# Five of eight row pairs with seven products in the feed-forward blocks of a two-layer decoder trunk

## The chip, the cores and the metric

The kernel runs on one core of a Trainium2 chip. The metric is the device time of one execution in microseconds (us); less is better. Engines are named as the profile names them: PE (TensorE, matmuls), DVE (VectorE), ACT (ScalarE), POOL (GpSimd) and SP (the engine that issues the transfers).

## The reference

A decoder trunk of two layers on 256 tokens of width 2048, all float32. Layer 0 mixes tokens with an mLSTM, layer 1 with an RG-LRU; behind each mixer stands a SwiGLU feed-forward block of inner width 5632, and a norm ends the trunk. The change lies in the feed-forward blocks:

```python
def swiglu(x, w_in, w_out):
    g, u = jnp.split(x @ w_in, 2, axis=-1)
    return (jax.nn.silu(g) * u) @ w_out

for layer in range(DEPTH):
    ...
    h = h + mix
    h = h + swiglu(rms_norm(h, norm_ffn[layer]), ffn_w_in[layer], ffn_w_out[layer])
return rms_norm(h, norm_final)
```

## The kernel before

Every float32 factor is kept as two halves: a high half, rounded by ACT (`hi`, L235), and a low half, the remainder made by DVE (`lo`, L236). A product of two factors is three matmuls, high by high, high by low and low by high, into the same accumulator (`product`, L752 to L755, one line for each).

`ffn` (L732) computes the feed-forward block of a layer in 11 blocks j of 512 inner columns. `inner` (L757) makes gate and up columns of a block for both halves of the tokens: `pairs` (L259) loads w_in in 8 row pairs p (two 128-row slices, gate and up columns, so a raw tile of 4 x 512 columns, two transfers of 512 KB), and each pair is a 2 x 2 by 2 x 2 block product. A plain pair does it in 8 products (24 matmuls). A pair in `SEVENS` does it in 7 products (21 matmuls, `PRODUCTS`, L35): for these, DVE first makes four sums of weight blocks into the one tile `sum` (L274, L277, L278), then both the three raw blocks that are used as they are (tiles `whix`, `wlox`, 1536 columns) and the four sums (`whit`, `wlot`, 2048 columns) are split into halves (`halves`, L238). The token side has its sums ready in tiles `p_f` (`NormPairs.pair`, L412), made once per layer while the mixer's output projection runs. Block 0 takes pairs 2 and 3 plainly (`BOTH`, L32), with additional token tiles from the pool `more`, since its pairs follow each other with nothing between them.

The halves lie in three high and three low tiles in rotation (`four`, L223); a plain pair takes one of each, a pair with seven products takes two. Raw tiles are also three in rotation, `sum` is one. So the tile of a pair's sums can be written when PE has read the raw blocks of the pair before, and the tile of raw blocks when PE has read the sums two tiles earlier.

Between the products of the pairs, PE does output pieces: `outs` (L816) multiplies the finished inner block j - 1 by w_out in 8 pieces of 12 matmuls, and `between` (L868) places one in each pair, from pair 4 of block j to pair 3 of block j + 1; so pairs 0 to 3 of block 1 have none of their own. A piece's weights are split by ACT and DVE too (`whio`, `wloo`), and ACT copies the residual into the accumulator (L855) and back (L862). At pair 6, the last with seven products, DVE and ACT combine the accumulators into gate and up (L787 to L801).

A scheduler sets each engine's order when the kernel is built: instructions in the program's order by readiness, those under `high_priority` earlier. Each engine then works through its order in sequence, waiting on semaphores; a waiting instruction holds up what stands behind it on its engine.

Of the kernel before, what the change touches and what calls it, by code (L numbers as in the profile page):

```python
# [28 lines left out]

SEVENS = (2, 3, 5, 6)  # L30

BOTH = (2, 3)  # L32

# [9 lines left out]
def kernel(  # L43
# [193 lines left out]

    def halves(name, src, n=4):  # L238

        hi, lo = four("whi", name, F32R, 3), four("wlo", name, F32R, 3)  # L240
        split(hi[:, 0:n, :], lo[:, 0:n, :], src[:, 0:n, :])
        return [(hi[:, i, :], lo[:, i, :]) for i in range(n)]
# [16 lines left out]
    def pairs(w, j):  # L259

        wv = w.rearrange("(k p) n -> p k n", p=P)
        for p in range(NK // 2):
# [9 lines left out]
            with tc.high_priority(offset=AHEAD):  # L272
                t = four("sum", f"{j}_{p}", F32, 1)
                nc.vector.tensor_tensor(  # L274
                    t[:, 0:2, :], raw[:, 1:3, :], raw[:, 3:4, :].broadcast_to([P, 2, NB]), op=ALU.add
                )
                nc.vector.tensor_tensor(t[:, 2, :], t[:, 0, :], raw[:, 2, :], op=ALU.add)  # L277
                nc.vector.tensor_tensor(t[:, 3, :], t[:, 2, :], raw[:, 0, :], op=ALU.add)  # L278
                both = halves(f"x{j}_{p}", raw, 3) + halves(f"t{j}_{p}", t)
            yield p, dict(zip(("B21", "B11", "B22", "T1", "T3", "T2", "T4"), both))  # L280
# [124 lines left out]
    class NormPairs(Norm):  # L405
# [6 lines left out]
        def pair(self, p):  # L412
# [7 lines left out]
            place, tag = ("c", "c") if "c" in pools else ("rawo", "raw0")  # L420
            c = pool_of(place).tile([P, 11 if place == "c" else 8, P], F32, tag=tag, name=f"c_{self.name}{p}")
            for k, sl in ((k0, slice(0, 2)), (k1, slice(2, 4))) if plain else ((k0, slice(1, 3)), (k1, slice(0, 4, 3))):
# [4 lines left out]
            else:  # L427

                nc.vector.tensor_tensor(
                    c[:, 4:6, :], c[:, 0:1, :].broadcast_to([P, 2, P]), c[:, 2:4, :], op=ALU.subtract  # L430
                )
                nc.vector.tensor_tensor(c[:, 6, :], c[:, 3, :], c[:, 4, :], op=ALU.subtract)
# [8 lines left out]
            if p in BOTH:  # L441

                nc.scalar.copy(c[:, 8, :], c[:, 0, :])
                nc.vector.tensor_tensor(c[:, 9, :], c[:, 1, :], c[:, 2, :], op=ALU.subtract)
                nc.vector.tensor_tensor(c[:, 10, :], c[:, 3, :], c[:, 0, :], op=ALU.subtract)
                more = pool_of("more").tile([P, 2, 3, P], F32R, tag=f"m{p}", name=f"m{p}_{self.name}")
                split(more[:, 0], more[:, 1], c[:, 8:11, :])
                self.more[p] = more
# [16 lines left out]
        def plain(self, p, f):  # L465

            x = self.x[p]
            if p not in self.more:
                return [(x[:, 0, i, :], x[:, 1, i, :]) for i in (2 * f, 2 * f + 1, 4 + f)]
            m = self.more[p]  # L470
            return [
                (t[:, 0, i, :], t[:, 1, i, :]) for t, i in (((x, 0), (x, 1), (m, 1)), ((x, 2), (m, 0), (m, 2)))[f]
            ]
# [258 lines left out]
    def ffn(layer, n, nxt):  # L732
# [24 lines left out]
        def inner(j, between):  # L757
# [12 lines left out]
            for p, ops in pairs(w, j):  # L770
# [14 lines left out]
                if p == SEVENS[-1]:  # L785
                    with tc.high_priority(offset=AHEAD):
                        nc.scalar.copy(s0, ps["P1"])  # L787
                        nc.vector.tensor_tensor(d0, ps["Q6"], s0, op=ALU.subtract)
                        nc.vector.tensor_tensor(d1, ps["P7"], d0, op=ALU.add)
            with tc.high_priority(offset=AHEAD):  # L790
                nc.vector.tensor_tensor(d0, ps["Q5"], d0, op=ALU.add)
                nc.vector.tensor_tensor(s1, ps["Q5"], d1, op=ALU.add)
                nc.vector.tensor_tensor(s0, ps["P2"], s0, op=ALU.add)
                nc.scalar.activation(s0, s0, AF.Silu, scale=n.rstd[:, 0:1])
                nc.vector.tensor_tensor(d0, ps["Q3"], d0, op=ALU.add)
                nc.vector.tensor_tensor(d1, ps["P4"], d1, op=ALU.subtract)
                nc.scalar.activation(d1, d1, AF.Silu, scale=n.rstd[:, 1:2])
# [317 lines left out]
```

## Time and profile before

| | |
|---|---|
| median of 3 runs | 2118.57 us (2117.81 to 2119.58) |
| the profiled execution's own time | 2118.39 us |
| its span, first to last instruction | 2116.6 us |
| PE busy | 2099.8 us, 99% |
| DVE busy | 1584.5 us, 75% |
| ACT busy | 1274.6 us, 60% |
| read from HBM | 401.84 MB, 191 GB/s over the span |

An engine's busy time is the union of its instructions' times. Matmuls overlap, so PE's busy share doesn't tell how far apart they are issued; for that the starts in the timeline, or the count of matmuls in a stretch, are read. Idle time of an engine that isn't waited for costs nothing. The stretches by stage: block 0 of the first feed-forward runs from 402.9 us, block 1 from 447.2, block 2 from 500.4, and from there each block takes 63.5 to 63.7 us; the second feed-forward begins at 1402.3 us and repeats the pattern.

### The profile page before, as it was taken

The page shows a single profiled execution, that of the slowest core. Times are in us where ns is not written, and L with a number is a line of the kernel's source. Part 1 is how long each engine was busy: PE and PEld are TensorE (multiplying, and loading weights), DVE is VectorE, ACT ScalarE, POOL GpSimd, SP SyncE. Part 2 cuts the span into 40 slices and gives each one's busy share as a digit, 9 for nine tenths or more (in the row PEclk, how much of TensorE's full clock was granted, in tenths as well). Part 3 has the DMA queues.
Part 4 walks back from the last instruction along what each step waited for, and adds up shares of the span by engine and source line. Part 5 has one row for each costly group of instructions (what it writes and reads, how often), then busy time and mean ns, then how long its engine had stood idle before and what let it go on. Part 6 is the DMA issues. An engine that isn't in the chain of part 4 may idle for free.

```text
span 2116.6 us, 27325 instructions
## 1 busy us (share of the span) xinstructions
PE 2099.8 (99%) x10604; PEld 1777.5 (84%) x10604; DVE 1584.5 (75%) x1610; ACT 1274.6 (60%) x1452; POOL 43.2 (2%) x62
## 2 busy tenths in 40 slices
PE   9999999999999999999999999999999999999998
PEld 8988888878888888888889999787888888888886
DVE  6655556688787787887776786868877877887875
ACT  5444445556666656666665758655756666666664
POOL 0011110000000000000000000000000000000002
PEclk9999999999999999999999999999999999999999
DMA  7556666556566565565545666765666655666653
GB/s 214 166 163 178 180 179 219 199 179 199 201 217 199 180 203 194 199 219 197 178 162 161 195 191 182 230 202 174 202 204 211 203 180 194 196 206 215 200 178 120
DMA packets 211082, 405.73 MB, mean 192 GB/s; under 512 B 14520, under 2 KB 14728, under 8 KB 210824
## 3 DMA queue, kind: packets, MB, share of 16 engines
q1 hardware_dynamic: 210808, 402.94, 59.0%
q8 instruction: 83, 1.36, 0.3%
q10 hardware_dynamic: 144, 1.05, 0.1%
q14 instruction: 47, 0.39, 0.0%
HBM read 401.84 MB, written 2.10 MB: 191 GB/s over the span
## 4 chain that ended last, share of the span: by engine, by line
PE 96%; ACT 2%; DVE 1%; issue 1%; DMA 0%; SPq 0%; ACTq 0%; POOLq 0%; POOL 0%; DVEq 0%
PE P L753 8%; PE out L753 8%; PE P L755 8%; PE P L754 8%; PE out L754 8%; PE out L755 8%; PE Q L754 7%; PE Q L755 7%; PE Q L753 7%; PE po L291 2%; PE po L292 2%; PE po L290 2%; PE qk L307 1%; PE qk L308 1%; PE qk L309 1%; PE v L290 1%
## 5 line engine op out<-in xcount | busy, mean ns | idle before, releaser
L211 DVE TENSOR_TENSOR wlo<-raw,whi 128x1024 fp32r<-128x1024 f32 (+1 forms) x225 | 273.1, 1217 | 179.9 <-ACT whi L210 178.7
L210 ACT CAST whi<-raw 128x1024 fp32r<-128x1024 f32 (+1 forms) x225 | 234.6, 1047 | 202.9 <-PE po L292 42.4
L236 DVE TENSOR_TENSOR wlot<-sum,whit 128x2048 fp32r<-128x2048 f32 x84 | 192.5, 2292 | 147.3 <-ACT whit L235 147.3
L753 PE MATMUL out<-whio,hh 128*128 128x512 f32 x704 | 275.0, 391 | 0.0
L754 PE MATMUL out<-wloo,hh 128*128 128x512 f32 x704 | 274.3, 390 | 0.0
L755 PE MATMUL out<-whio,hh 128*128 128x512 f32 x704 | 273.3, 389 | 0.0
L235 ACT CAST whio<-rawo 128x1024 fp32r<-128x1024 f32 (+1 forms) x166 | 183.7, 1106 | 126.5 <-PE out L755 119.1
L862 ACT COPY h<-out 128x512 f32<-128x512 f32 x154 | 90.2, 586 | 252.5 <-PE out L755 252.5
L236 DVE TENSOR_TENSOR wlo<-raw,whi 128x2048 fp32r<-128x2048 f32 x92 | 210.3, 2288 | 32.0 <-ACT whi L235 31.4
L236 DVE TENSOR_TENSOR wloo<-rawo,whio 128x1024 fp32r<-128x1024 f32 (+1 forms) x166 | 210.9, 1282 | 3.6 <-ACT whio L235 3.0
L235 ACT CAST whit<-sum 128x2048 fp32r<-128x2048 f32 x84 | 160.5, 1911 | 74.2 <-DVE sum L278 36.0
L235 ACT CAST whi<-raw 128x2048 fp32r<-128x2048 f32 x92 | 175.6, 1916 | 29.5 <-DMA raw<-in_ffn_w_in_dram 18.5
L236 DVE TENSOR_TENSOR wlox<-raw,whix 128x1536 fp32r<-128x1536 f32 x84 | 147.3, 1753 | 47.8 <-ACT whix L235 47.8
L753 PEld LDWEIGHTS out<-whio,hh 128*128 128x128 f32 x704 | 132.2, 188 | 28.9 <-ACT out L855 0.9
L755 PEld LDWEIGHTS out<-whio,hh 128*128 128x128 f32 x704 | 132.2, 188 | 27.8
L754 PEld LDWEIGHTS out<-wloo,hh 128*128 128x128 f32 x704 | 132.2, 188 | 27.2
L753 PE MATMUL P<-whi,p_f 128*128 128x512 f32 x364 | 141.9, 390 | 1.6 <-ACT whi L235 1.6
L755 PE MATMUL P<-whi,p_f 128*128 128x512 f32 x364 | 141.9, 390 | 0.0
L754 PE MATMUL P<-wlo,p_f 128*128 128x512 f32 x364 | 141.6, 389 | 0.0
L753 PE MATMUL Q<-whi,p_f 128*128 128x512 f32 x356 | 140.6, 396 | 0.2 <-DVE h L485 0.2
L754 PE MATMUL Q<-wlo,p_f 128*128 128x512 f32 x356 | 138.8, 390 | 0.0
L755 PE MATMUL Q<-whi,p_f 128*128 128x512 f32 x356 | 138.6, 389 | 0.0
(284 smaller groups left out, 4819.0 us busy)
## 6 DMA issues: line engine op xcount, KB each, us to landing
raw<-in_ffn_w_in_dram SPq DMA_DIRECT2D x352, 512.0 KB, 4.9
rawo<-in_ffn_w_out_dram SPq DMA_DIRECT2D x176, 512.0 KB, 4.3
raw<-in_m_w_in_dram SPq DMA_DIRECT2D x95, 512.0 KB, 3.8
raw<-in_r_w_in_dram SPq DMA_DIRECT2D x64, 512.0 KB, 3.8
raw<-in_m_w_out_dram SPq DMA_DIRECT2D x32, 512.0 KB, 3.7
raw<-in_r_w_out_dram SPq DMA_DIRECT2D x32, 512.0 KB, 3.9
gr<-in_r_gate_w_dram SPq DMA_DIRECT2D x8, 512.0 KB, 3.9
h<-in_x_dram SPq DMA_DIRECT2D x4, 512.0 KB, 7.7
```

The lines of the kernel that those rows point to most:

```text
L210: nc.scalar.copy(hi[:, i:i + step, 0:ncols], r)
L211: nc.vector.tensor_tensor(lo[:, i:i + step, 0:ncols], r, hi[:, i:i + step, 0:ncols].bitcast(F32), op=ALU.subtract)
L235: nc.scalar.copy(hi, src)
L236: nc.vector.tensor_tensor(lo, src, hi.bitcast(F32), op=ALU.subtract)
L290: nc.tensor.matmul(o, lhsT=ah[:, bs], rhs=hi, start=(k == 0), stop=False)
L291: nc.tensor.matmul(o, lhsT=ah[:, bs], rhs=lo, start=False, stop=False)
L292: nc.tensor.matmul(o, lhsT=al[:, bs], rhs=hi, start=False, stop=(k == nk - 1))
L307: nc.tensor.matmul(o, lhsT=hi, rhs=ah, start=first_in_bank, stop=False, skip_group_check=True)
L753: nc.tensor.matmul(o, lhsT=a[0], rhs=b[0], start=start, stop=False, **kw)
L754: nc.tensor.matmul(o, lhsT=a[0], rhs=b[1], start=False, stop=False, **kw)
L755: nc.tensor.matmul(o, lhsT=a[1], rhs=b[0], start=False, stop=stop, **kw)
L862: nc.scalar.copy(hs, o)
```

## The change

Pair 4 joins the pairs with seven products in all blocks but block 0, where it stays plain, like pairs 2 and 3, from tiles in `more`. The low and high halves of the four sums are made in two parts of two sums each (`step=2`): T1 and T3 first, then T2 and T4. On the token side the difference that two products share is kept with the other sign (A7), so that one tile less is needed in `more`, and the signs of `d1` are turned to match.

```diff
--- before.py
+++ after.py
@@ -27,9 +27,9 @@
 BIG = 1e30
 AHEAD = 1000
 
-SEVENS = (2, 3, 5, 6)
-
-BOTH = (2, 3)
+SEVENS = (2, 3, 4, 5, 6)
+
+BOTH = (2, 3, 4)
 
 SHIFT = 48
 PRODUCTS = (
@@ -235,10 +235,12 @@
         nc.scalar.copy(hi, src)
         nc.vector.tensor_tensor(lo, src, hi.bitcast(F32), op=ALU.subtract)
 
-    def halves(name, src, n=4):
+    def halves(name, src, n=4, step=4):
 
         hi, lo = four("whi", name, F32R, 3), four("wlo", name, F32R, 3)
-        split(hi[:, 0:n, :], lo[:, 0:n, :], src[:, 0:n, :])
+        for i in range(0, n, step):
+            at = slice(i, min(n, i + step))
+            split(hi[:, at, :], lo[:, at, :], src[:, at, :])
         return [(hi[:, i, :], lo[:, i, :]) for i in range(n)]
 
     def stream4(w, c0, nk):
@@ -276,7 +278,7 @@
                 )
                 nc.vector.tensor_tensor(t[:, 2, :], t[:, 0, :], raw[:, 2, :], op=ALU.add)
                 nc.vector.tensor_tensor(t[:, 3, :], t[:, 2, :], raw[:, 0, :], op=ALU.add)
-                both = halves(f"x{j}_{p}", raw, 3) + halves(f"t{j}_{p}", t)
+                both = halves(f"x{j}_{p}", raw, 3) + halves(f"t{j}_{p}", t, step=2)
             yield p, dict(zip(("B21", "B11", "B22", "T1", "T3", "T2", "T4"), both))
 
     def linear_tok(w, c0, nk, act, name, ncols=NB, lag=0):
@@ -418,7 +420,7 @@
             for i, (k, b) in enumerate(order):
                 nc.tensor.transpose(pt[:, i, :], h[:, b, k * P:(k + 1) * P], ident)
             place, tag = ("c", "c") if "c" in pools else ("rawo", "raw0")
-            c = pool_of(place).tile([P, 11 if place == "c" else 8, P], F32, tag=tag, name=f"c_{self.name}{p}")
+            c = pool_of(place).tile([P, 10 if place == "c" else 8, P], F32, tag=tag, name=f"c_{self.name}{p}")
             for k, sl in ((k0, slice(0, 2)), (k1, slice(2, 4))) if plain else ((k0, slice(1, 3)), (k1, slice(0, 4, 3))):
                 nc.scalar.activation(c[:, sl, :], pt[:, sl, :], AF.Copy, scale=self.gain[:, k:k + 1])
             if plain:
@@ -426,9 +428,8 @@
                 src = c[:, 0:6, :]
             else:
 
-                nc.vector.tensor_tensor(
-                    c[:, 4:6, :], c[:, 0:1, :].broadcast_to([P, 2, P]), c[:, 2:4, :], op=ALU.subtract
-                )
+                nc.vector.tensor_tensor(c[:, 4, :], c[:, 0, :], c[:, 2, :], op=ALU.subtract)
+                nc.vector.tensor_tensor(c[:, 5, :], c[:, 3, :], c[:, 0, :], op=ALU.subtract)
                 nc.vector.tensor_tensor(c[:, 6, :], c[:, 3, :], c[:, 4, :], op=ALU.subtract)
                 nc.vector.tensor_tensor(c[:, 7, :], c[:, 1, :], c[:, 6, :], op=ALU.subtract)
                 src = c[:, 1:8, :]
@@ -442,9 +443,8 @@
 
                 nc.scalar.copy(c[:, 8, :], c[:, 0, :])
                 nc.vector.tensor_tensor(c[:, 9, :], c[:, 1, :], c[:, 2, :], op=ALU.subtract)
-                nc.vector.tensor_tensor(c[:, 10, :], c[:, 3, :], c[:, 0, :], op=ALU.subtract)
-                more = pool_of("more").tile([P, 2, 3, P], F32R, tag=f"m{p}", name=f"m{p}_{self.name}")
-                split(more[:, 0], more[:, 1], c[:, 8:11, :])
+                more = pool_of("more").tile([P, 2, 2, P], F32R, tag=f"m{p}", name=f"m{p}_{self.name}")
+                split(more[:, 0], more[:, 1], c[:, 8:10, :])
                 self.more[p] = more
 
         def parts(self, q):
@@ -469,7 +469,7 @@
                 return [(x[:, 0, i, :], x[:, 1, i, :]) for i in (2 * f, 2 * f + 1, 4 + f)]
             m = self.more[p]
             return [
-                (t[:, 0, i, :], t[:, 1, i, :]) for t, i in (((x, 0), (x, 1), (m, 1)), ((x, 2), (m, 0), (m, 2)))[f]
+                (t[:, 0, i, :], t[:, 1, i, :]) for t, i in (((x, 0), (x, 1), (m, 1)), ((x, 2), (m, 0), (x, 4)))[f]
             ]
 
     def bc2(ap):
@@ -786,14 +786,15 @@
                     with tc.high_priority(offset=AHEAD):
                         nc.scalar.copy(s0, ps["P1"])
                         nc.vector.tensor_tensor(d0, ps["Q6"], s0, op=ALU.subtract)
-                        nc.vector.tensor_tensor(d1, ps["P7"], d0, op=ALU.add)
+
+                        nc.vector.tensor_tensor(d1, ps["P7"], d0, op=ALU.subtract)
             with tc.high_priority(offset=AHEAD):
                 nc.vector.tensor_tensor(d0, ps["Q5"], d0, op=ALU.add)
-                nc.vector.tensor_tensor(s1, ps["Q5"], d1, op=ALU.add)
+                nc.vector.tensor_tensor(s1, ps["Q5"], d1, op=ALU.subtract)
                 nc.vector.tensor_tensor(s0, ps["P2"], s0, op=ALU.add)
                 nc.scalar.activation(s0, s0, AF.Silu, scale=n.rstd[:, 0:1])
                 nc.vector.tensor_tensor(d0, ps["Q3"], d0, op=ALU.add)
-                nc.vector.tensor_tensor(d1, ps["P4"], d1, op=ALU.subtract)
+                nc.vector.tensor_tensor(d1, ps["P4"], d1, op=ALU.add)
                 nc.scalar.activation(d1, d1, AF.Silu, scale=n.rstd[:, 1:2])
                 for b, (u, g) in enumerate(((d0, s0), (s1, d1))):
                     nc.vector.scalar_tensor_tensor(
```

What the built order of instructions shows at three places (a name carries the tile's kind, then block and pair, then a buffer number: `wlot8_5` is the low half of the sums of pair 5 in block 8):

DVE in an ordinary block, first before, from the sums of pair 5 on:

```order
L274 TENSOR_TENSOR sum8_5_7492<-raw8_5_7489 128x1024
L277 TENSOR_TENSOR sum8_5_7492<-sum8_5_7492,raw8_5_7489 128x512
L278 TENSOR_TENSOR sum8_5_7492<-sum8_5_7492,raw8_5_7489 128x512
L236 TENSOR_TENSOR wlo8_4_7435<-raw8_4_7431,whi8_4_7434 128x2048
L236 TENSOR_TENSOR wlox8_5_7497<-raw8_5_7489,whix8_5_7496 128x1536
L236 TENSOR_TENSOR wloo700_7458<-rawo700_7456,whio700_7457 128x1024
L236 TENSOR_TENSOR wloo701_7464<-rawo701_7462,whio701_7463 128x1024
L236 TENSOR_TENSOR wlot8_5_7501<-sum8_5_7492,whit8_5_7500 128x2048
```

and with the change, from the sums of pair 4 on:

```order
L276 TENSOR_TENSOR sum8_4_7557<-raw8_4_7554 128x1024
L279 TENSOR_TENSOR sum8_4_7557<-sum8_4_7557,raw8_4_7554 128x512
L280 TENSOR_TENSOR sum8_4_7557<-sum8_4_7557,raw8_4_7554 128x512
L236 TENSOR_TENSOR wlox8_4_7562<-raw8_4_7554,whix8_4_7561 128x1536
L236 TENSOR_TENSOR wlot8_4_7566<-sum8_4_7557,whit8_4_7565 128x1024 x2
L236 TENSOR_TENSOR wloo700_7588<-rawo700_7586,whio700_7587 128x1024
L276 TENSOR_TENSOR sum8_5_7622<-raw8_5_7619 128x1024
L236 TENSOR_TENSOR wloo701_7594<-rawo701_7592,whio701_7593 128x1024
L279 TENSOR_TENSOR sum8_5_7622<-sum8_5_7622,raw8_5_7619 128x512
L236 TENSOR_TENSOR wlox8_5_7627<-raw8_5_7619,whix8_5_7626 128x1536
L280 TENSOR_TENSOR sum8_5_7622<-sum8_5_7622,raw8_5_7619 128x512
L236 TENSOR_TENSOR wlot8_5_7631<-sum8_5_7622,whit8_5_7630 128x1024 x2
```

The single 2048-wide split of pair 4 has become three sums, a 1536-wide split and two 1024-wide splits, and every `wlot` is now two instructions.

PE at the end of block 0, from the first product with the sums of pair 6 (`P7`, `Q5`, `Q6`, `P4` are accumulators), before:

```order
L753 MATMUL P7_0_3881<-whit0_6_3906,p6_f0_3708 128x512
L753 MATMUL Q5_0_3669<-whit0_6_3906,p6_f0_3708 128x512
L753 MATMUL Q6_0_3888<-whit0_6_3906,p6_f0_3708 128x512
L753 MATMUL P4_0_3690<-whit0_6_3906,p6_f0_3708 128x512
L753 MATMUL P2_0_3676<-whi0_7_3937,p7_f0_3751 128x512
L754 MATMUL P7_0_3881<-wlot0_6_3907,p6_f0_3708 128x512
L755 MATMUL P7_0_3881<-whit0_6_3906,p6_f0_3708 128x512
L754 MATMUL Q5_0_3669<-wlot0_6_3907,p6_f0_3708 128x512
```

and with the change:

```order
L753 MATMUL P7_0_3893<-whit0_6_3918,p6_f0_3718 128x512
L754 MATMUL P7_0_3893<-wlot0_6_3919,p6_f0_3718 128x512
L755 MATMUL P7_0_3893<-whit0_6_3918,p6_f0_3718 128x512
L753 MATMUL Q5_0_3678<-whit0_6_3918,p6_f0_3718 128x512
L754 MATMUL Q5_0_3678<-wlot0_6_3919,p6_f0_3718 128x512
L755 MATMUL Q5_0_3678<-whit0_6_3918,p6_f0_3718 128x512
L753 MATMUL Q6_0_3900<-whit0_6_3918,p6_f0_3718 128x512
L754 MATMUL Q6_0_3900<-wlot0_6_3919,p6_f0_3718 128x512
```

Before, the four products begin with the high half alone, and a matmul of pair 7 stands ahead of the first low half; now each product runs its three matmuls in sequence.

ACT in an ordinary block, around the copies of an output piece (`L862`, later `L863`), before:

```order
L235 CAST whi8_4_7434<-raw8_4_7431 128x2048
L235 CAST whix8_5_7496<-raw8_5_7489 128x1536
L235 CAST whio700_7457<-rawo700_7456 128x1024
L862 COPY h_73<-out631_7407 128x512
L235 CAST whio701_7463<-rawo701_7462 128x1024
L855 COPY out700_7468<-h_73 128x512
L235 CAST whit8_5_7500<-sum8_5_7492 128x2048
```

and with the change, in block 7, where the rotation of the three tiles stands differently:

```order
L235 CAST whix7_4_7075<-raw7_4_7068 128x1536
L235 CAST whit7_4_7079<-sum7_4_7071 128x1024
L235 CAST whio600_7101<-rawo600_7100 128x1024
L863 COPY h_73<-out531_7044 128x512
L235 CAST whit7_4_7079<-sum7_4_7071 128x1024
L235 CAST whio601_7107<-rawo601_7106 128x1024
L856 COPY out600_7112<-h_73 128x512
L235 CAST whix7_5_7140<-raw7_5_7133 128x1536
```

In that block the second part of the copy of pair 4's sums stands behind the copy of output piece `out531`; in the blocks beside it both parts stand ahead of it.

## Rows read from the trace of the kernel before

**Rows 1.** The page: busy time by engine, and the chain by engine.

```profile
PE 2099.8 (99%) x10604; PEld 1777.5 (84%) x10604; DVE 1584.5 (75%) x1610; ACT 1274.6 (60%) x1452; POOL 43.2 (2%) x62
...
PE 96%; ACT 2%; DVE 1%; issue 1%; DMA 0%; SPq 0%; ACTq 0%; POOLq 0%; POOL 0%; DVEq 0%
```

**Rows 2.** Busy time by stretch: block 1, block 8, its pairs 2 to 6.

```profile
core 0: us, PE busy (x) PEld busy (x) DVE busy (x) ACT busy (x) POOL busy (x), PEclk, DMA share, GB/s
...
447.20:500.40 53.20, 53.20 (x238) 43.19 (x236) 48.19 (x42) 31.81 (x30) 0.00 (x0) 1.00 0.59 195
881.97:945.62 63.65, 63.65 (x285) 52.52 (x284) 51.21 (x44) 40.55 (x42) 0.00 (x0) 1.00 0.61 198
899.45:937.49 38.04, 38.04 (x169) 31.27 (x168) 30.31 (x22) 25.84 (x25) 0.00 (x0) 1.00 0.64 203
```

**Rows 3.** Timelines (start, duration, engine, line, [idle before, releaser]): block 8, pair 6.

```profile
926.94 2.29 DVE L236 TENSOR_TENSOR wlot<-sum,whit 128x2048 fp32r<-128x2048 f32 x1 [0.71 <-ACT whit L235]
...
932.50 0.39 PE L754 MATMUL P<-wlot,p_f 128*128 128x512 f32 x1
```

**Rows 4.** Timelines: block 1, sums of pairs 3, 5 and 6, DVE then PE.

```profile
468.63 2.29 DVE L236 TENSOR_TENSOR wlot<-sum,whit 128x2048 fp32r<-128x2048 f32 x1
...
477.23 2.29 DVE L236 TENSOR_TENSOR wlot<-sum,whit 128x2048 fp32r<-128x2048 f32 x1 [0.69 <-ACT whit L235]
...
488.86 2.28 DVE L236 TENSOR_TENSOR wlot<-sum,whit 128x2048 fp32r<-128x2048 f32 x1
...
470.98 0.50 PE L754 MATMUL P<-wlot,p_f 128*128 128x512 f32 x1
...
479.74 0.40 PE L754 MATMUL P<-wlot,p_f 128*128 128x512 f32 x1
...
491.33 0.39 PE L754 MATMUL P<-wlot,p_f 128*128 128x512 f32 x1
```

**Rows 5.** Groups by line and shape, DVE (busy us, mean ns | idle, releasers).

```profile
L236 DVE TENSOR_TENSOR wlo<-raw,whi 128x2048 fp32r<-128x2048 f32 x92 | 210.3, 2288 | 32.0 <-ACT whi L235 31.4 <-DMA raw<-in_ffn_w_in_dram 0.4
L236 DVE TENSOR_TENSOR wlot<-sum,whit 128x2048 fp32r<-128x2048 f32 x84 | 192.5, 2292 | 147.3 <-ACT whit L235 147.3
L236 DVE TENSOR_TENSOR wloo<-rawo,whio 128x1024 fp32r<-128x1024 f32 x156 | 188.1, 1218 | 1.3 <-ACT whio L235 0.8
L236 DVE TENSOR_TENSOR wlox<-raw,whix 128x1536 fp32r<-128x1536 f32 x84 | 147.3, 1753 | 47.8 <-ACT whix L235 47.8
L274 DVE TENSOR_TENSOR sum<-raw 128x1024 f32<-128x1024 f32 x84 | 102.4, 1219 | 1.3
L277 DVE TENSOR_TENSOR sum<-sum,raw 128x512 f32<-128x512 f32 x84 | 57.8, 688 | 1.7
L278 DVE TENSOR_TENSOR sum<-sum,raw 128x512 f32<-128x512 f32 x84 | 57.7, 687 | 1.4
```

**Rows 6.** The same view, ACT.

```profile
L235 ACT CAST whi<-raw 128x2048 fp32r<-128x2048 f32 x92 | 175.6, 1916 | 29.5 <-DMA raw<-in_ffn_w_in_dram 18.5 <-PE P L755 7.9
L235 ACT CAST whio<-rawo 128x1024 fp32r<-128x1024 f32 x156 | 164.6, 1055 | 123.8 <-PE out L755 116.6 <-DMA rawo<-in_ffn_w_out_dram 5.0
L235 ACT CAST whit<-sum 128x2048 fp32r<-128x2048 f32 x84 | 160.5, 1911 | 74.2 <-DVE sum L278 36.0 <-PE P L755 19.7 <-PE Q L755 16.8
L235 ACT CAST whix<-raw 128x1536 fp32r<-128x1536 f32 x84 | 124.6, 1483 | 5.0 <-PE P L755 1.0
```

**Rows 7.** Timelines: end of block 0, ACT, PE, then PE in the second layer.

```profile
435.54 1.92 ACT L235 CAST whit<-sum 128x2048 fp32r<-128x2048 f32 x1 [2.74 <-DVE sum L278]
...
438.59 0.39 PE L753 MATMUL P<-whit,p_f 128*128 128x512 f32 x1
439.79 0.50 PE L753 MATMUL P<-whi,p_f 128*128 128x512 f32 x1 [0.81 <-ACT whi L235]
...
1439.71 0.50 PE L753 MATMUL P<-whi,p_f 128*128 128x512 f32 x1 [0.83 <-ACT whi L235]
```

**Rows 8.** Timeline of DVE: end of the mixer's output projection, first layer.

```profile
402.44 0.69 DVE L485 TENSOR_TENSOR h<-po,h 128x512 f32<-128x512 f32 x1 [7.89 <-PE po L292]
```

## The prediction

> **What bounds the kernel now.** I read the page's engine shares and its chain of waits first, then busy time by stage, the groups of instructions by shape, and last the timelines of TensorE (PE), ScalarE (ACT) and VectorE (DVE) at three places. PE is busy 99% of the span and carries 96% of the chain [rows 1]: a matmul taken out of the order is worth one step of that order, if the operands of the matmuls behind it are ready in time. The step is not the 390 ns that a matmul's row shows, because these overlap: in the stretch of four seven-product pairs and one plain pair, 84 + 24 product matmuls and five output pieces of 12 fill 38.04 us [rows 2], so a step is 38.04 / 168 = 0.2264 us. The granted clock there is 1.00, the 2.4 GHz level.
>
> DVE is second. In an ordinary block (block j of the eleven, j from 2 up) it is busy 51.21 of 63.65 us; in block 1 it is busy 48.19 of 53.20 us, since the first four pairs of that block have no output piece between them [rows 2]. What the readers must see is the margin, the time from the end of a low half on DVE to the matmul that first reads it. In an ordinary block the sums of pair 6 are ready at 926.94 + 2.29 = 929.23 and read at 932.50, a margin of 3.3 us [rows 3]. In block 1 the three margins are 0.1, 0.2 and 0.2 us (470.92 to 470.98, 479.52 to 479.74, 491.14 to 491.33) [rows 4]: there the two engines end together.
>
> **The change, part by part.** (1) Matmuls. Pair 4 goes from 8 products to 7 in ten blocks of two layers, three matmuls each: 20 x 3 = 60, which is what the built order shows as a difference in count. All lie on PE's path: 60 x 0.2264 = 13.6 us less.
>
> (2) Work for DVE and ACT, per block. Pair 4 trades one plain split (2.288) for three sums (1.219 + 0.688 + 0.687), a 1536-wide split (1.753) and the split of the sums in two parts (2 x 1.218): 6.78 - 2.29 = 4.49 us more. The other four seven-product pairs pay 2 x 1.218 - 2.292 = 0.14 us each for the two parts, 0.58 together. DVE: 5.07 us more per block [rows 5]. ACT: 1.483 + 2 x 1.055 - 1.916 + 4 x (2 x 1.055 - 1.911) = 2.5 us more [rows 6]; with 40.55 us busy of 63.65 [rows 2] it has room.
>
> (3) Ordinary blocks (2 to 10, 18 in all). DVE goes to 51.21 + 5.07 = 56.3 of 63.65 - 0.68 = 63.0 us. In the run of pairs 2 to 6 it goes from 30.31 of 38.04 [rows 2] to 35.4 of 37.4 us, so it loses ground: per pair its work is 6.78 plus one output split of 1.22, 8.0 us, and PE's time is 33 steps, 7.5 us. Five such pairs cost 2.5 us of the 3.3 us margin, and the pairs 7, 0 and 1 behind them give it back. The products with T1 and T3 also come first and need only the first part, which ends 1.2 us before the second. So I take no stall. The cover is thin: where it breaks, each us of lag in a block is one us of PE, 18 times.
>
> (4) Block 1. DVE's 48.19 + 5.07 = 53.26 us meet PE's 53.20 - 0.68 = 52.52: 0.74 us too much, with no margin to eat. From below the stall is nothing (if the earlier first parts hide it), from above all idle time stays: 0.74 + (53.20 - 48.19) = 5.75 us. I take 0.74 plus a quarter of the 5.01 us idle, 2.0 us, because the small margins say that DVE waits little there; two layers, 4.0 us.
>
> (5) End of block 0. PE stands still there because ACT's copy of the sums waits 2.74 us for the last of three sums, and the copy of pair 7 is queued behind it: 439.79 - 438.59 - 0.23 = 0.97 us, and about the same in the second layer (0.83 us by its wait alone) [rows 7]. With two parts the first copy needs only the first sum, and the order built for the change has the products of pair 6 in plain sequence again. I take back both gaps in full, 1.9 us. From below: nothing.
>
> (6) Norm tiles. Pair 4 makes five more small DVE operations per layer, pairs 2 and 3 a smaller extra tile: about 1 us of DVE, in a stage where DVE then waits 7.89 us for the output projection [rows 8]. Nothing; without that cover 1 us per layer. The signs of d1 and A7 change operations, not counts. Transfers and their bytes stay, with the DMA engines busy 0.64 of the run of pairs [rows 2]; pair 4's raw tile is held up to DVE's added 4.5 us longer, and three raw tiles rotate, so the load of pair 7 that takes its place has two pairs of PE's time, 15 us, in hand.
>
> Sum: 2118.39 (the profiled execution; the median is 2118.57) - 13.6 + 4.0 - 1.9 = **2106.9 us**.
>
> One rule speaks about (3) and (4). The rows show DVE late in block 1 while it is busy 75% over the span [rows 1, 4]. The Trainium skill ("Perfetto Trace Analysis", Identifying the Most-Contended Engine) takes occupancy of VectorE as a fair measure of its headroom; by it nothing would stall and the sum would be 2102.9. The margins of block 1 disagree: an average over the span hides that block.
>
> **The rivals.** *A: no new stall at all.* The two parts bring the first products forward by 1.2 us, more than the 0.74 us that block 1 is short. Against: its margins of 0.1 to 0.2 us. 2118.39 - 13.6 - 1.9 = 2102.9.
>
> *B: every third block stumbles.* A block now takes 13 tiles from the three in rotation instead of 12, so ACT's order differs from block to block. In three of ten blocks per layer the second part of the sums stands behind the copy of an output piece, and everything to pair 7 slides. Against: that part is first read after the piece. If it costs 1.5 us in 6 blocks: 2106.9 + 9 = 2115.9; at half of that, 2111.4.
>
> *C: DVE becomes the pace, slower than before.* The place is the run of pairs 2 to 6. Before, DVE is idle 38.04 - 30.31 = 7.73 us in it, waiting for ACT's copies, which wait for PE to release tiles [rows 5, 6]. If those waits keep their length, the run needs 35.4 + 7.7 = 43.1 us against PE's 37.4, 5.7 late; less the 3.3 us margin, 2.4 us per block. 18 x 2.4 = 43, and 2 x 5.75 = 11.5 for block 1: 2118.4 - 13.6 + 54.7 = 2159. It decides from where more than 2.0 + 3.3 = 5.3 us of the idle time remains. Against: a wait in front of an engine that was early shrinks as it gets late.
>
> That the change does not do what it says is ruled out by the count of 60 and by blocks that keep all other products.
>
> **How the numbers follow.** Forecast 0.64, A 0.20, B 0.11, C 0.05. The range holds A's 2102.9 and block 1 at 4 us in each layer without the gain at block 0 (2118.39 - 13.6 + 8 = 2112.8): 2102 to 2113, which leaves out C, half of B and the forecast's upper tail. A measurement of this kernel can tell about 0.2%, 4.2 us: faster means under 2114.3. Forecast (less 0.02 for its upper tail), A and half of B: 0.88. The rest of these, 0.07, is no change; C is slower, 0.05.
>
> **What would show it.** Right: 60 fewer matmuls; ordinary blocks 0.68 us shorter, 63.0 us, without PE waits; DVE at 56 us in them; block 1 between 52.5 and 55 us with small gaps at the sums; the 0.97 us gap at the end of block 0 gone. Wrong: ordinary blocks as long as before, with PE waiting for DVE at pairs 4 to 6 (C), or in every third block at pair 7 (B); block 1 above 58 us; or a step other than 0.226 us.

## The result, and the profile after

The changed kernel takes 2103.97 us in the median of 6 runs (2102.56 to 2105.72) beside 2118.27 us for the kernel before (2117.81 to 2119.58); the ratio is 0.9934, interval 0.9923 to 0.9944. Its profiled execution is the slowest of the six: 2105.72 us, span 2103.9 us.

The page of the changed kernel, busy time by engine:

```profile
PE 2087.6 (99%) x10544; PEld 1766.2 (84%) x10544; DVE 1673.3 (80%) x1808; ACT 1313.5 (62%) x1580; POOL 43.2 (2%) x62
```

Against [rows 1]: 60 matmuls fewer, and DVE busy 80% instead of 75%; the shares of the chain by engine are the same as there, PE 96%. Busy time by stretch, block 1, block 2 and block 8 of the first layer:

```profile
core 0: us, PE busy (x) PEld busy (x) DVE busy (x) ACT busy (x) POOL busy (x), PEclk, DMA share, GB/s
447.22:499.87 52.65, 52.65 (x234) 42.47 (x233) 48.94 (x48) 30.70 (x32) 0.00 (x0) 1.00 0.58 191
499.87:563.86 63.99, 63.60 (x283) 51.81 (x281) 59.76 (x56) 44.91 (x51) 0.00 (x0) 1.00 0.64 206
878.54:941.54 63.00, 63.00 (x282) 51.95 (x281) 56.23 (x53) 42.56 (x48) 0.00 (x0) 1.00 0.63 206
```

Block 8 went from 63.65 us [rows 2] to 63.00, DVE in it from 51.21 to 56.23; the other blocks from 3 on take 62.85 to 63.00 us in both layers. Block 1 went from 53.20 [rows 2] to 52.65 us without a wait of PE, although 5.07 us of work were added for it: the window's DVE time rose by 0.75 us only. Most of the rest stands in block 2, where DVE is busy 59.76 us beside 56.23 in block 8; it shows in DVE's timeline around the first sums of that block. Before the change:

```profile
510.70 2.29 DVE L236 TENSOR_TENSOR wlot<-sum,whit 128x2048 fp32r<-128x2048 f32 x1 [2.82 <-ACT whit L235]
```

and with it (DVE, then PE at the first output piece of block 2):

```profile
503.23 1.21 DVE L236 TENSOR_TENSOR wloo<-rawo,whio 128x1024 fp32r<-128x1024 f32 x1
...
510.60 1.22 DVE L236 TENSOR_TENSOR wlot<-sum,whit 128x1024 fp32r<-128x1024 f32 x1
...
504.50 0.50 PE L754 MATMUL out<-wloo,hh 128*128 128x512 f32 x1 [0.16 <-DVE wloo L236]
...
506.61 0.50 PE L754 MATMUL out<-wloo,hh 128*128 128x512 f32 x1 [0.23 <-DVE wloo L236]
```

DVE reached the first low half of block 2's output piece late (PE steps of 0.55 and 0.62 us there, from 503.95 and 505.99), but 7 us later, at 510.6, it began the first part of the sums about as early as the whole before (10.7 us after the block's start, before 10.3), and the 2.82 us that it used to wait for ACT were gone. I read this so: the excess of block 1 is worked off in that wait. A run below tests it. In the second layer block 2 takes 63.03 us and shows no such step.

At the end of block 0 the gap of [rows 7] is gone in the second layer (that block: 44.77 to 43.89 us). In the first it moved to another place (44.27 to 44.23 us); ACT, then PE:

```profile
432.84 1.05 ACT L235 CAST whio<-rawo 128x1024 fp32r<-128x1024 f32 x1 [4.03 <-DMA rawo<-in_ffn_w_out_dram]
433.80 1.47 ACT L235 CAST whix<-raw 128x1536 fp32r<-128x1536 f32 x1
...
437.11 0.50 PE L754 MATMUL P<-wlox,p_f 128*128 128x512 f32 x1 [0.79 <-DVE wlox L236]
```

In the new order the copy of the first output weights stands ahead of pair 6's raw blocks on ACT and waits 4.03 us for its transfer.

### The profile page after: what moved, and what is told of

The parts are those of the page before. It is cut to its first block, busy times and chain, and to the rows that moved or that the text cites. A ratio compares the mean times of both kernels' runs of the same rounds, so it can differ in the third digit from the quotient of the medians.

```text
span 2103.9 us, 27554 instructions
## 1 busy us (share of the span) xinstructions
PE 2087.6 (99%) x10544; PEld 1766.2 (84%) x10544; DVE 1673.3 (80%) x1808; ACT 1313.5 (62%) x1580; POOL 43.2 (2%) x62
## 3 DMA queue, kind: packets, MB, share of 16 engines
q10 hardware_dynamic: 144, 1.05, 0.1%
## 4 chain that ended last, share of the span: by engine, by line
PE 96%; ACT 2%; DVE 1%; issue 1%; DMA 0%; SPq 0%; ACTq 0%; POOLq 0%; POOL 0%; DVEq 0%
PE P L753 8%; PE P L754 8%; PE P L755 8%; PE out L753 8%; PE out L754 7%; PE out L755 7%; PE Q L753 6%; PE Q L754 6%; PE Q L755 6%; PE po L293 2%; PE po L292 2%; PE po L294 2%; PE qk L309 1%; PE qk L310 1%; PE qk L311 1%; PE v L292 1%
## 5 line engine op out<-in xcount | busy, mean ns | idle before, releaser
L236 DVE TENSOR_TENSOR wlot<-sum,whit 128x1024 fp32r<-128x1024 f32 x208 | 249.3, 1219 | 72.0 <-ACT whit L235 72.0
L235 ACT CAST whit<-sum 128x1024 fp32r<-128x1024 f32 x208 | 213.7, 1051 | 93.7 <-PE Q L755 30.1
L863 ACT COPY h<-out 128x512 f32<-128x512 f32 x154 | 90.2, 586 | 186.4 <-PE out L755 186.3
L236 DVE TENSOR_TENSOR wlox<-raw,whix 128x1536 fp32r<-128x1536 f32 x104 | 182.4, 1754 | 22.4 <-ACT whix L235 22.1
L236 DVE TENSOR_TENSOR wlo<-raw,whi 128x2048 fp32r<-128x2048 f32 x72 | 164.2, 2287 | 23.4 <-ACT whi L235 23.3
L235 ACT CAST whi<-raw 128x2048 fp32r<-128x2048 f32 x72 | 137.0, 1915 | 40.5 <-DMA raw<-in_ffn_w_in_dram 26.2
L235 ACT CAST whix<-raw 128x1536 fp32r<-128x1536 f32 x104 | 154.2, 1483 | 10.6 <-PE P L755 7.6
L276 DVE TENSOR_TENSOR sum<-raw 128x1024 f32<-128x1024 f32 x104 | 127.1, 1222 | 5.0 <-DMA raw<-in_ffn_w_in_dram 3.0
L755 PE MATMUL P<-whi,p_f 128*128 128x512 f32 x282 | 110.0, 390 | 0.0
L753 PE MATMUL Q<-whi,p_f 128*128 128x512 f32 x276 | 109.7, 398 | 0.2 <-DVE h L485 0.2
L753 PE MATMUL P<-whi,p_f 128*128 128x512 f32 x282 | 109.7, 389 | 0.0
L754 PE MATMUL P<-wlo,p_f 128*128 128x512 f32 x282 | 109.7, 389 | 0.0
```

Of the source, the lines that this page charges most:

```text
L235: nc.scalar.copy(hi, src)
L236: nc.vector.tensor_tensor(lo, src, hi.bitcast(F32), op=ALU.subtract)
L276: nc.vector.tensor_tensor(t[:, 0:2, :], raw[:, 1:3, :], raw[:, 3:4, :].broadcast_to([P, 2, NB]), op=ALU.add)
L753: nc.tensor.matmul(o, lhsT=a[0], rhs=b[0], start=start, stop=False, **kw)
L754: nc.tensor.matmul(o, lhsT=a[0], rhs=b[1], start=False, stop=False, **kw)
L755: nc.tensor.matmul(o, lhsT=a[1], rhs=b[0], start=False, stop=stop, **kw)
```

## The experiments

All kernels start from the changed one; its median is 2104.0 us. The kernel before, run beside them, had medians of 2117.6 to 2118.5 us.

### What the two parts do

Parts alone, without the fifth pair:

```diff
-SEVENS = (2, 3, 4, 5, 6)
+SEVENS = (2, 3, 5, 6)
-BOTH = (2, 3, 4)
+BOTH = (2, 3)
```

> Pair 4 is plain again (SEVENS 2, 3, 5, 6), the sums are still made in two parts. Theory (the gain is the 60 matmuls; the parts only repair the end of block 0): 0 to 1.9 us below the kernel before, 2116.4 to 2118.3 us, the 0.97 us gap at the end of block 0 gone in at least one layer, the margins of pairs 3 and 6 in block 1 up from 0.1 and 0.2 us to over 1 us. Rival (the parts themselves pay): 2 to 6 us faster than before. Rival (the parts cost DVE 0.14 x 84 = 12 us and that shows): slower than before.

Measured: 2115.96 us (10 runs), ratio to before 0.999, 0.998 to 0.9999. That is 2.5 us under the kernel before, just outside the theory's range and at the lower end of the first rival's. Blocks 0 and 1 are 43.8 and 52.9 us long, in both layers together 1.4 us less than before for block 0 and 0.6 us less for block 1; the others have not changed. Alone, the parts are worth about 2 us, and not at the end of block 0 only.

The fifth pair without parts:

```diff
-                both = halves(f"x{j}_{p}", raw, 3) + halves(f"t{j}_{p}", t, step=2)
+                both = halves(f"x{j}_{p}", raw, 3) + halves(f"t{j}_{p}", t)
```

> The changed kernel with the sums split in one part (step 4): pair 4 keeps its seven products. Theory (the parts are what kept block 1 free of stalls): blocks 0 and 1 lose 1 to 3 us in each layer, ordinary blocks stay at 63.0 us, 2106 to 2110 us. Rival (block 1's excess of DVE work is simply carried into the plain pairs behind it and the parts do nothing): 2104 us, within 1 us of the changed kernel. Rival (margins of ordinary blocks break): above 2115 us.

Measured: 2133.36 us (4 runs), ratio 1.0078, 1.0059 to 1.0097. That is far outside what my theory allowed, in the second rival's range, and slower than before the change: the same 60 matmuls are gone, yet the kernel takes 29 us more than the changed one. Stretches of that kernel, block 1 and block 5 of the first layer:

```profile
448.58:504.70 56.12, 53.39 (x234) 42.45 (x233) 51.37 (x46) 33.48 (x31) 0.00 (x0) 1.00 0.56 190
694.59:760.30 65.71, 64.07 (x283) 51.56 (x281) 59.01 (x52) 41.83 (x43) 0.00 (x0) 1.00 0.60 199
```

and PE's largest waits in the feed-forward blocks of that kernel (us in total, times, longest):

```profile
PE P L754 <- DVE wlox L236: 2.7, 6, 0.8
PE P L753 <- ACT whi L235: 2.2, 2, 1.1
PE Q L753 <- DVE ds L793: 1.8, 4, 0.5
PE P L753 <- DVE ds L794: 1.8, 2, 1.2
```

Block 1 takes 3.5 us more than in the changed kernel (5.0 in the second layer, where the granted clock is 0.50 for some 3 us of it), and in blocks 5 and 8, each third one, PE waits at their start for `ds`, the combining of the accumulators of the block before: instructions of DVE that are now queued late. Two runs split the loss by place:

```diff
-                both = halves(f"x{j}_{p}", raw, 3) + halves(f"t{j}_{p}", t, step=2)
+                both = halves(f"x{j}_{p}", raw, 3) + halves(f"t{j}_{p}", t, step=2 if j < 2 else 4)
```

> The sums split in two parts in blocks 0 and 1 only, whole from block 2 on. In the run without any parts, 12.0 of the 25.8 us lost lie in blocks 0 and 1 of the two layers and 13.8 us in the blocks behind them. If the parts work block by block (each block loses what its own sums cost it): 2104 + 14, 2116 to 2120 us, blocks 0 to 1 as long as in the changed kernel, and single blocks of 64 to 66 us behind them. Rival: the late start of the layer was carried into the later blocks; then blocks 2 to 10 lose at most 2 us per layer, 2104 to 2108 us.

Measured: 2119.28 us (10 runs), ratio 1.0007, 0.9997 to 1.0017. Blocks 0 and 1 are back at 43.9 and 52.7 us, the others take 63.3 to 63.6 us (62.85 to 63.00 in the changed kernel), and blocks 5 and 8, with the wait at their start, 65.1 and 65.7 (64.9 both in the second layer). Block 8 of the first layer:

```profile
880.67:946.36 65.69, 64.07 (x282) 51.76 (x282) 59.10 (x53) 42.04 (x43) 0.00 (x0) 1.00 0.61 200
```

The counterpart, in two parts from block 2 on:

```diff
-                both = halves(f"x{j}_{p}", raw, 3) + halves(f"t{j}_{p}", t, step=2)
+                both = halves(f"x{j}_{p}", raw, 3) + halves(f"t{j}_{p}", t, step=2 if j > 1 else 4)
```

> The counterpart of the run with parts in blocks 0 and 1 only: sums whole in blocks 0 and 1, in two parts from block 2 on. That run came to 2119.3 us, 15 us above the changed kernel, with blocks 0 and 1 of 42.9 to 52.7 us as in the changed kernel. If the parts work block by block, the losses of the two runs add up to that of the run without any parts (2133.4 - 2104.0 = 29): here 2104 + 12 to 14, 2115 to 2119 us, blocks 0 and 1 of 45.7 and 56 to 57.5 us, the others at 63.0. Rival: a lag built up in blocks 0 and 1 is not made good and blocks 2 to 10 are longer too, above 2121 us.

Measured: 2116.24 us (10 runs), ratio 0.9992, 0.9982 to 1.0002. Block 1 of each layer, and block 2 of the first:

```profile
448.17:504.27 56.10, 53.40 (x235) 42.42 (x234) 51.36 (x46) 33.27 (x31) 0.00 (x0) 1.00 0.55 189
1446.32:1504.02 57.70, 55.02 (x235) 43.56 (x233) 51.31 (x46) 33.27 (x31) 0.00 (x0) 0.97 0.54 184
504.27:567.27 63.00, 63.00 (x283) 51.95 (x282) 57.91 (x54) 42.31 (x47) 0.00 (x0) 1.00 0.62 204
```

What block 1 loses isn't carried on: block 2 takes 63.00 us. The two losses, 15.3 and 12.3 us, make 27.6 of the 29.4 us. So the parts work block by block, and without them the fifth pair is a loss. In block 1 they are worth 3.4 and 5.0 us; of the 5.0 an estimated 1.5 belong to the clock (57.70 us against 56.10), which was granted at 0.50 from 1476.2 to 1479.2 us, while block 1 of the first layer held 1.00. The parts bring the first halves forward, and with them the built order of DVE and PE becomes another one; these runs do not tell the two apart.

### How much more VectorE can take

The third sum of each pair made twice in blocks 2 to 10 (the result stays the same):

```diff
+                for _ in range(1 if j > 1 else 0):
+                    nc.vector.tensor_tensor(t[:, 3, :], t[:, 2, :], raw[:, 0, :], op=ALU.add)
```

> The changed kernel with the third sum made twice in blocks 2 to 10: 0.69 us more of DVE per pair with seven products, 3.4 us a block, the result unchanged; DVE 59.7 of 63.0 us. Theory (idle time of DVE shrinks as DVE gets late, so the margins take it): 2104 to 2108 us, at most 1 us lost in every third block, where the margin at pair 7 was 1.9 us. Rival (DVE already sets the pace in the run of pairs 2 to 6): each added us is lost, 18 x 3.4 = 62 us, 2166 us.

Measured: 2106.01 us (4 runs), ratio 0.9945, 0.9928 to 0.9961. A block of it:

```profile
687.28:750.28 63.00, 63.00 (x282) 51.95 (x281) 59.71 (x60) 42.42 (x48) 0.00 (x0) 1.00 0.61 202
```

DVE is busy 59.71 of 63.00 us and PE waits nowhere in it; in all, 2 us are lost, as the theory had it. Then made three times (`range(2 if j > 1 else 0)`):

> The changed kernel with the third sum made three times in blocks 2 to 10: 6.9 us more for VectorE per block, 56.3 + 6.9 = 63.2 us in blocks of 63.0 us (no result changes). With one repetition (59.7 us busy) the blocks stayed at 63.0 us. Theory (VectorE's lag is free up to nearly full occupancy, and from there each us is one us of PE): blocks of 63.5 to 65 us, 2113 to 2140 us. Rival (the room is not used up even now, because the repeated sums fall into waits): below 2110 us. Second rival (the waits of VectorE for ScalarE's copies stay, as in case C of the prediction): blocks of 66 us and more, above 2150 us.

Measured: 2128.47 us (4 runs), ratio 1.0051, 1.0038 to 1.0065. A block of the second layer, and PE's waits:

```profile
1693.09:1757.17 64.08, 63.83 (x282) 51.55 (x281) 60.84 (x63) 42.12 (x48) 0.00 (x0) 1.00 0.59 196
```

```profile
PE P L756 <- DVE wlo L236: 3.9, 16, 0.3
```

Here the room ends, as the theory had it: blocks of 63.9 to 64.1 us, one of 64.6. DVE stays idle 3.2 us of 64.1 even though PE now waits for it in almost each block. The step from free to costly lies between 3.4 and 6.9 us more per block.

The same doubling in block 1 alone (`range(1 if j == 1 else 0)`):

> The changed kernel with the third sum of each of the five pairs made twice in block 1 alone, 3.4 us more for VectorE there in each layer (48.9 + 3.4 of 52.7 us, with 3.7 us idle; no result changes). By the prediction's step (every us that VectorE has too much in block 1 is one us of PE, since the margins there are 0.1 to 0.6 us): 3 to 3.4 us per layer, 2109.5 to 2111 us, the loss inside block 1. By the reading of the changed kernel's trace (the excess is carried into block 2 and used up in VectorE's wait of 2.4 to 2.9 us in front of the second pair's sums, output pieces being placed ahead meanwhile): at most 1.5 us per layer, 2104 to 2107 us, the loss at the first output pieces of block 2.

Measured: 2112.38 us (8 runs), ratio 0.9973, 0.9962 to 0.9983. My reading of the trace falls: block 1 takes 57.98 and 56.50 us, 5.3 and 3.8 more, and block 2 takes 62.99 and 63.04, where the changed kernel has 63.99 and 63.03. Nothing more is carried over. The loss lies where the prediction's step puts it, inside block 1, and is larger than the 3 to 3.4 us per layer that the step gives. Stretches of the first layer, block 1 and 2.3 us in it:

```profile
445.55:503.53 57.98, 55.90 (x235) 43.15 (x233) 53.60 (x55) 33.01 (x35) 0.00 (x0) 0.97 0.51 174
...
492.50:494.80 2.30, 2.30 (x7) 1.82 (x6) 2.30 (x3) 2.14 (x2) 0.00 (x0) 0.50 1.07 406
```

PE first waits 1.3 us for ACT's copy of pair 7, and behind that twice 0.2 us; then the granted clock is 0.50 for some 2 us. The second layer's block 1 has the same waits without the half clock, which accounts for the 1.5 us between the two.

### Another engine, and a sixth pair

The third sum on GpSimd:

```diff
-                nc.vector.tensor_tensor(t[:, 3, :], t[:, 2, :], raw[:, 0, :], op=ALU.add)
+                nc.gpsimd.tensor_tensor(t[:, 3, :], t[:, 2, :], raw[:, 0, :], op=ALU.add)
```

> The changed kernel with the third sum of each pair on GpSimd instead of VectorE: 0.69 us less for VectorE per pair, 3.4 us per block, against 1.63 us for the same shape on GpSimd. Theory (VectorE has room since its lag is absorbed by output pieces that are placed ahead): no change, 2102 to 2106 us. Rival 1: VectorE's load is still what delays block 2 and the blocks at the start: 2100 to 2102. Rival 2: the longer way over GpSimd makes the second part of the sums late, or VectorE's own instructions get longer beside it (mean of the first sum above 1.25 us): above 2107 us.

Measured: 2120.64 us (10 runs), ratio 1.0009, 1.0000 to 1.0019: the second rival. Rows of DVE's splits and of GpSimd's sums:

```profile
L236 DVE TENSOR_TENSOR wlot<-sum,whit 128x1024 fp32r<-128x1024 f32 x208 | 280.4, 1362 | 93.3 <-ACT whit L235 92.1
...
L280 POOL TENSOR_TENSOR sum<-sum,raw x104: 1285/2679/4324, 420.8 to 2056.5; 128x512 f32<-128x512 f32 x104
...
L236 DVE TENSOR_TENSOR wlot<-sum,whit x208: 1207/1224/2324, 428.7 to 2060.3; 128x1024 fp32r<-128x1024 f32 x104
...
L1061 POOL TENSOR_TENSOR y<-h,gf x6: 1289/1295/3277, 2096.0 to 2106.9; 128x512 f32<-128x512 f32 x6
```

In the last three rows the three figures are the shortest, the median and the longest, in ns. The sum takes 1.29 us at the shortest on GpSimd, but 2.68 us in the median, and DVE's split of the sums takes 1.36 us in the mean instead of 1.22, single ones up to 2.32. The 1.63 us that I had expected was the mean of six such instructions as in the last row, of which one, beside a split of DVE, takes 3.28 us. The sign that I had named, a first sum above 1.25 us, does not show: that instruction stays at 1.22 us, and the splits get longer. Later blocks bear it (62.8 to 63.1 us); block 1 does not (57.4 and 61.4 us; the second holds 6.4 us, 1495.1 to 1501.5, at a granted clock of 0.50).

Pair 7 as a sixth pair (three small parameter tiles moved to make room):

```diff
-SEVENS = (2, 3, 4, 5, 6)
+SEVENS = (2, 3, 4, 5, 6, 7)
...
-                        (c, seven[a], ops[b], p == SEVENS[-1] and c in ("P7", "P1", "Q6")) for c, a, b in PRODUCTS
+                        (c, seven[a], ops[b], p == SEVENS[-1] and (c in ("P7", "P1", "Q6") or p == NP - 1)) for c, a, b in PRODUCTS
```

> Pair 7 takes seven products too, in all blocks, block 0 included: 66 matmuls fewer than in the changed kernel, 66 x 0.2264 = 14.9 us; DVE gains about 4.6 us a block, 60.9 of 62.3 us. Theory (a margin of 1.9 us or more is left, and each further pair in a row costs 0.5 us of it): most of it is kept in ordinary blocks, some is lost in blocks 0 and 1 and at the joint to the next block, 2090 to 2098 us. Rival (DVE sets the pace from here): no gain, 2103 us or more, with PE waiting for DVE in ordinary blocks.

Measured: 2168.69 us (4 runs), ratio 1.0235, 1.022 to 1.025: slower than before the change, and PE does wait for DVE in ordinary blocks. PE's waits:

```profile
PE out L754 <- DVE wloo L236: 15.4, 14, 1.2
PE out L753 <- ACT out L856: 10.7, 8, 1.3
PE P L753 <- DVE ds L794: 8.0, 2, 4.1
...
PE tr_f L421 <- DVE h L485: 2.9, 1, 2.9
```

Now no plain pair stands behind the last one with seven products. The combining of the accumulators, which it covered, comes at the block's end: PE waits 4.1 us there in block 0, and in later blocks for the output piece that follows. The last row is another matter: the feed-forward of the first layer began 5.5 us late, at 408.5 us, with the transposes of the norm ordered ahead of its first products. Part of the loss is the clock's: its mean over the span is 0.989 beside 0.997 in the changed kernel, by which I estimate up to 17 us (0.008 of 2163). To take the sixth pair elsewhere, I put pair 1 (and, since its accumulators need their banks, both transposes of the previous block behind pair 0):

```diff
-SEVENS = (2, 3, 4, 5, 6)
+SEVENS = (1, 2, 3, 4, 5, 6)
-BOTH = (2, 3, 4)
+BOTH = (1, 2, 3, 4)
...
-                if turns:
+                while turns and p == 0:
```

> Six pairs in seven products, the sixth being pair 1 (pair 7, plain, stays the last), outside block 0; the transposes of the previous block's result both go behind pair 0. 60 matmuls fewer than the changed kernel, 13.6 us. VectorE gets 4.6 us more per block: 60.9 of 62.3 us. Theory (what cost 65 us in the run with pair 7 as the sixth was the end of the block, where nothing covers the folding of the three accumulators, not VectorE's load): 2091 to 2100 us. Rival: VectorE's load itself is too much at 60.9 us per block; then blocks of 63 to 65 us, 2106 us and more, with PE waiting for VectorE in every block.

Measured: 2113.4 us (8 runs), ratio 0.9976, 0.9965 to 0.9986: neither number. Ordinary blocks take 62.2 to 63.9 us, near the 62.3 aimed at, but block 1 takes 56.9 and 57.0 us, and the first layer again begins at 409.3 instead of 403.0 us.

The same with the third sums on GpSimd:

> As the run before, with the third sum of each of the six pairs on GpSimd: VectorE at 60.9 - 6 x 0.69 = 56.8 us per block, where the changed kernel has 56.3. Theory: 2104 - 13.6, 2089 to 2094 us, blocks of 62.2 us. Rival: if pair 1 or the moved transposes cost time by their place and not by VectorE's load, it is no faster than the run before. Second rival: GpSimd's 1.63 us delay the second parts, above 2097 us.

Measured: 2176.39 us (4 runs), ratio 1.0276, 1.0260 to 1.0291. Blocks of 63.6 to 66.8 us, above the second rival's 2097 us. DVE is busy 1754.6 us in this run and 1748.9 in the one before, although 124 sums have left it: the splits beside GpSimd take up what was saved.

Last, the sixth pair only from block 2 on, and the parameter tiles in the pool `x`, at the other end of memory, against the kernel with pair 1:

```diff
-        return p not in SEVENS or j == 0 and p in BOTH
+        return p not in SEVENS or j == 0 and p in BOTH or j == 1 and p == 1
...
-            if j == 0:
+            if j == 1:
                 close_pools("more")
...
-                while turns and p == 0:
+                for _ in range(min(len(turns), 1 if j == 1 or p else 2)):
...
-    rows = [pool_of("y").tile(...
+    rows = [(pool_of("x") if i >= 0 else const).tile(...
```

> Six pairs in seven products (1 to 6) in blocks 2 to 10, five in block 1 (pair 1 plain there), and the small parameter tiles kept on the other side of memory. In the run with six pairs in block 1 too, block 1 lost 4 us per layer and the first layer started 6.3 us late, because the first weights' place overlapped other memory than before and the transposes of the norm were ordered ahead of the first products. Theory (both are places of their own, VectorE's 60.9 of 62.3 us in ordinary blocks costs little): 54 matmuls less than the changed kernel, 12.2 us, and 3 to 7 us for the waits at the transposes of the previous block, 2095 to 2099 us, first layer starting at 403 us, block 1 below 54 us. Rival: the load of VectorE only shows where it has lost its lead, and takes that lead in block 2 instead: block 2 of 66 us and more, in all 2101 us and more.

Measured: **2095.74 us** (4 runs, 2094.10 to 2097.19), ratio to before 0.9895, 0.9880 to 0.9910: faster than both kernels, 8.2 us under the changed one. Its page, two stretches (blocks 2 and 7 of the first layer) and PE's largest wait in the feed-forward:

```profile
PE 2073.4 (99%) x10490; PEld 1754.0 (84%) x10490; DVE 1740.0 (83%) x1908; ACT 1332.5 (64%) x1620; POOL 43.3 (2%) x62
```

```profile
497.97:560.21 62.24, 62.24 (x279) 51.43 (x278) 60.37 (x60) 42.69 (x50) 0.00 (x0) 1.00 0.59 203
810.51:873.45 62.94, 62.44 (x280) 51.43 (x278) 59.12 (x58) 44.35 (x51) 0.00 (x0) 1.00 0.59 201
```

```profile
PE P L753 <- DVE hh L496: 2.5, 6, 0.6
```

The first layer begins at 401.5 us and block 1 takes 52.7 us, so both losses of the run with pair 1 were places of their own. Of the 12.2 us that 54 matmuls give, 4 do not show in the time. The waits at the previous block's transposes make up most of them: the row has 2.5 us, and measured from the start of one matmul to the next these six stops take 3.5 us.

## Why the prediction was right, and where it was not

**The sum.** Forecast 2106.9, measured 2103.97, inside the range; of the cases, A (2102.9) lies nearer than the forecast. The terms, from block lengths in both layers:

| step | forecast | measured |
|---|---|---|
| (1) 60 matmuls | -13.6 | -13.7: blocks 3 to 10 are 0.69 shorter in the mean |
| (4) block 1, and what it leaves to block 2 | +4.0 | +1.3 (0.24 in block 1, 1.04 in block 2) |
| (5) block 0 | -1.9 | -0.9 (0.04 and 0.88) |
| outside blocks 0 to 10 | 0 | +0.7 in the profiled execution |

The profiled execution lies 1.75 us above the median, which makes up the rest. That the sum came so close is partly luck: (4) was 2.7 us too high, (5) and what lies outside the blocks 1.7 us too low.

**(1), (2), (3).** Right, and (2) nearly to the digit: DVE at 56.23 us where 56.3 were worked out, the 1024-wide split at 1.219 us. The margin of pair 6 behaved better than (3) had it. DVE and PE in block 8:

```profile
922.13 2.35 DVE L236 TENSOR_TENSOR wlot<-sum,whit 128x1024 fp32r<-128x1024 f32 x2
...
928.17 0.39 PE L754 MATMUL P<-wlot,p_f 128*128 128x512 f32 x1
```

Both parts are ready at 924.48 and read from 928.17 on, 3.7 us later (4.8 after the first part) where [rows 3] had 3.3 and the step left 0.8. The step holds two figures that don't agree: 35.4 us of DVE in 37.4 us leave room, while five times 8.0 in five times 7.5 us lose ground; the first is the nearer one (34.5 in 37.7 us, in the row shown under the rivals). The cover was not thin: 3.4 us more fitted in (e4_dve1), 6.9 did not, and then a block lost 1.05 us (e13_dve2). That a broken cover would cost in all 18 blocks was right; that it would cost one for one is not shown.

**(4) failed in its size.** The step took DVE's whole time in the window as due in the window, added a quarter of the idle time, and left PE 2.0 us short per layer. The chip shows 0.12 us in block 1 and 1.0 and 0.05 us in block 2. Its mechanism holds: the next 3.4 us cost 3.8 and 5.3 us (e12_dve_block1), 1.5 of the 5.3 at the half clock, so block 1 has no room left; the change just fits. What makes it fit is what case A named, the parts: without them block 1 takes 3.4 and 5.0 us more (e10_parts_later). The small margins of [rows 4] were no measure of it. From pair 3 on they are 0.1 to 0.6 us in the changed kernel too, with 5 us more work and without a wait of PE. That other products, placed between by the built order, cover them is my reading and was not tested.

**(5)** was right in the second layer (0.88 us). In the first, what was late next had not been named: a copy that waits for a transfer, ahead of pair 6 on ACT.

**The rivals.** *B* did not happen: in its blocks the first part still has a margin of 2.7 us at pair 6, where the blocks beside them have 4.8. Without parts it does happen, in blocks 5 and 8, at 1.5 to 2.3 us above their neighbours against the 1.5 us assumed, at `ds` and not at pair 7 (e5_parts01). *C* needed more than 5.3 us of DVE's idle time to stay in the run of pairs 2 to 6. The same run in block 8 of the changed kernel:

```profile
895.70:933.38 37.68, 37.68 (x168) 30.97 (x167) 34.50 (x30) 28.10 (x30) 0.00 (x0) 1.00 0.66 209
```

Of 7.7 us of idle time 3.2 are left, so the waits shrank as the argument against C had it. With 6.9 us more work (e13_dve2) the whole block keeps 3.2 us of it, and 2128 us were measured there, under C's 2159.

**The rule on occupancy.** DVE's share was 80% in the changed kernel, 78% without parts and 80% with the doubled sums in block 1; the times are 2104.0, 2133.4 and 2112.4 us. The Trainium skill ("Perfetto Trace Analysis", Identifying the Most-Contended Engine) calls that share a fair measure of how close the engine is to its limit. Read as the prediction reads it, nothing would stall in any of the three; that met the number of the change (2102.9 against 2104.0) and missed the two others.

## What to carry to other kernels

Whether a second engine stands in the way was decided here by when its work is ready in each block, not by its share of the span: two instructions of half the width cost 0.14 us more per pair and turned a loss of 15 us into a gain of 14. An engine's wait inside a window is room only once, so try the next dose too, in the stage that is tight and in the ordinary one apart. When a larger version loses, look where: the kernel with pair 1 as the sixth lost more than its gain of 13.6 us in block 1 (8.6 us in both layers) and at one late start (6.3), and without these two it was the fastest.

## What was not expected of the hardware

- After short waits PE ran at half clock: in e12_dve_block1 the granted clock is 0.50 from 492.5 to 494.8 us, the 1.2 GHz level, and matmuls follow each other in 0.427 us instead of 0.2264. The second layer has the same waits without it, and its block 1 is 1.5 us shorter (56.50 against 57.98): waits of 1.7 us together cost another 1.5 us in the one layer and nothing in the other.
- GpSimd and DVE held each other up (e7_pool): GpSimd's sum takes 1.29 us at the shortest and 2.68 in the median, DVE's splits 1.36 instead of 1.22 us in the mean. Two meetings in block 8 of the first layer, DVE first in the one and GpSimd in the other:

```profile
889.07 1.75 DVE L236 TENSOR_TENSOR wlox<-raw,whix 128x1536 fp32r<-128x1536 f32 x1
...
889.29 2.68 POOL L280 TENSOR_TENSOR sum<-sum,raw 128x512 f32<-128x512 f32 x1 [22.59 <-DVE sum L279]
...
897.65 1.29 POOL L280 TENSOR_TENSOR sum<-sum,raw 128x512 f32<-128x512 f32 x1 [5.69 <-DVE sum L279]
...
897.81 3.35 DVE L236 TENSOR_TENSOR wloo<-rawo,whio 128x1024 fp32r<-128x1024 f32 x2 [0.29 <-ACT whio L235]
```

  The one that begins first keeps its usual length. The sum that begins second ends 1.15 us after the split, the two splits that begin second take 3.35 us together, where two take 2.35 undisturbed. The Trainium skill ("SBUF — State Buffer", SBUF: two separate sides) says that a DVE operation with two inputs in SBUF and a GpSimd operation that reads it take a shared pair of ports by turns, each for a whole instruction. The rows agree: each of the late ones is longer by nearly what was left of the other (1.4 of 1.5 us, 1.0 of 1.1).
- Moving three tiles of 512 bytes per partition, which are used at the start alone, made the first feed-forward begin 5.5 to 6.3 us later (e3_six, e8_six_low); in e8_six_low the granted clock is 0.50 from 406.5 to 412.9 us, across that start. At the other end of memory they cost nothing (e11_six_from2). That other overlaps of memory, and so another order, are the cause is argued from that one move; the tile that collides was not looked for.
